# The last feed-forward product kept by tokens instead of by features, at the end of a two-block model

## The chip, the cores and the metric

The kernel runs on one core of a Trainium2 chip. Its metric is the device time of one execution in microseconds (us), the median of several runs. The core has five engines that run beside each other, each with its own queue in order: TensorE (PE in the profile, its weight loads PEld) multiplies matrices, VectorE (DVE) and ScalarE (ACT) work element by element, GpSimd (POOL) does a few small operations and issues some DMAs, SyncE (SP) issues most of the DMAs.

## The reference, cut to what matters

The model is two blocks on one sequence of 512 tokens with 1024 features, all in float32. Only the end of the second block is touched by the change:

```
h  = rms_norm(x, ffn_pre_g)
gt, up = split(h @ w_gate_up)            # 1024 -> 2 x 2816
f  = (silu(gt) * up) @ w_down            # 2816 -> 1024
x  = x + rms_norm(f, ffn_post_g)         # a norm per token over 1024 features
return x
```

## The kernel before, in words

**Layout.** Nearly everything is kept by features: a tile holds 128 features in its partitions and the 512 tokens in its columns, so 1024 features are eight tiles. The host hands in x transposed and transposes the output back (`outT`, 1024 x 512).

**Products.** A float32 product is done as three TensorE products of a rounded high part and a low part (`mm3`, lines 149 to 152). `gemm_tile` (line 154) makes one output tile of 128 features: for each 128 rows of the contraction it loads the weights as the stationary operand and passes the activations, 512 tokens wide, as the moving one. Weights come in blocks of up to 8 x 128 columns (`wblock`, line 143): SP loads the block to `wr`, ACT casts it to `wh` (line 138), DVE subtracts to get `wl` (line 139). There are three buffers each of `wr`, `wh` and `wl`. `gemm_tok` (line 180) is another form, used early in the kernel: there the activations are stationary, 128 tokens at a time, and the weights move, 512 columns wide.

**Order.** The program is written as one straight line and a planner (the tile framework) puts each engine's instructions in order by priority; weight blocks have a priority of 300 instructions ahead (`WPRI`). A buffer that is still in use makes the next writer wait in its engine's queue.

**The feed-forward part (lines 1089 to 1154).** The 44 tiles of gate and up take 24 matmuls each of 512 columns. Each pair gives one hidden tile (`hid`, high and low part `uh`, `ul`). The hidden tiles are made in two groups of eleven. After the first group eight output tiles get the first half of the contraction, 33 matmuls of 512 columns each, and are copied to `fo`. After the second group the token range is cut in two halves of 256: for each half the eight output tiles get the rest, 33 matmuls of 256 columns each, so each weight block of that group is loaded and split twice. Then comes the norm of the half: squares of the eight tiles are summed by ACT and DVE, `col_sum` (line 217) sums them over the partitions by small matmuls (line 223), `rsqrt_col` (line 227) gives one column per 128 tokens, the power on POOL (line 231), `row_bc` (line 234) spreads the columns to a row by four passes of TensorE (line 238), ACT copies it out (line 256), and two DVE operations per output tile (lines 1152 and 1153) scale it and add the residual `h`. The output leaves in 128 KB DMAs (line 1154). The norm of the first half is put off so that it lies beside the matmuls of the second.

Of the kernel before, what the change touches and what calls it, by code (L numbers as in the profile page):

```python
# [6 lines left out]
F32 = mybir.dt.float32  # L7
# [9 lines left out]
P = 128  # L17
S = 512
# [20 lines left out]
X1 = 0  # L39
X2 = 30  # L40
X3 = 40
TLATE = 30
APRI = 60
BPRI = 120

# [23 lines left out]
def _build(tc, nc, es, a, out):  # L69
# [58 lines left out]
    def vcol(name, i=0, n=1):  # L128
        c, k = VEC[name]
        assert i + n <= k  # L130
        return vec[:, c + i:c + i + n]
# [22 lines left out]
    def gemm_tile(src_blocks, xs, n=S):  # L154

        ps = acc.tile([P, S], F32, tag="acc", name="acc")
        k0, tot = 0, sum(nk for _, nk in src_blocks)
        for src, nk in src_blocks:
            wh, wl = wblock(src, nk)
            for k in range(nk):  # L160
                xh, xl = xs[k0]
                mm3(ps[:, :n], wh[:, k, :], wl[:, k, :], xh, xl, k0 == 0, k0 == tot - 1)
                k0 += 1
        return ps
# [43 lines left out]
    def sq_acc(accum, k, src, scale=1.0):  # L208
        if k == 0:
            A.activation(out=accum, in_=src, func=AF.Square, scale=scale)  # L210
        else:
            sq = nrm.tile([P, S], F32, tag="sq", name="sq")
            n = accum.shape[-1]
            A.activation(out=sq[:, :n], in_=src, func=AF.Square, scale=scale)
            V.tensor_tensor(out=accum, in0=accum, in1=sq[:, :n], op=ALU.add)
# [872 lines left out]

    with ExitStack() as ec:
        pc = ec.enter_context(pool("pf2", 2, reuse_waits="tile"))  # L1090
        ph2 = ec.enter_context(pool("phid2", 11, reuse_waits="tile"))
        fo = [None] * 8

        def gu_tiles(ns):

            pss, ws = [], []
            for n in ns:
                pss.append(acc.tile([P, S], F32, tag="acc", name="acc"))
                ws.append(wblock(a["w_gu"][n]))
            for cl in parts:  # L1100
                for ps, (wh, wl) in zip(pss, ws):
                    for k in range(8):
                        mm3(ps[:, cl], wh[:, k, :], wl[:, k, :], xs[k][0][:, cl], xs[k][1][:, cl], k == 0, k == 7)
            return pss

        order = [n for i in range(22) for n in (i, 22 + i)]

        early = {}
        for n, ps in zip(order, gu_tiles(order[:3]) + [gemm_tile([(a["w_gu"][n], 8)], xs) for n in order[3:NEARLY]]):
            early[n] = pc.tile([P, S], F32, tag=f"e{n}", name="early", bufs=1)  # L1110
            A.copy(out=early[n], in_=ps)
        for cl in parts:
            r3(cl, HF)

        def gu(n):
            return early[n] if n in early else gemm_tile([(a["w_gu"][n], 8)], xs)

        for grp in range(2):
            hid = []
            for n in range(11 * grp, 11 * grp + 11):  # L1120
                ps = gu(n)
                t = pc.tile([P, S], F32, tag="t", name="t")
                V.tensor_tensor(out=t, in0=ps, in1=R3, op=ALU.mult)
                A.activation(out=t, in_=t, func=AF.Silu)
                ps = gu(22 + n)
                t2 = pc.tile([P, S], F32, tag="t2", name="t2")
                V.tensor_tensor(out=t2, in0=ps, in1=R3, op=ALU.mult)
                V.tensor_tensor(out=t2, in0=t2, in1=t, op=ALU.mult)
                hid.append(split_act(t2, pl=ph2, tag="u"))
            o = grp * 11  # L1130
            if grp == 0:
                for n in range(8):
                    w = a["w_dn"][n]
                    ps = gemm_tile([(w[:, o:o + 8, :], 8), (w[:, o + 8:o + 11, :], 3)], hid)
                    fo[n] = pso.tile([P, S], F32, tag=f"so{n}", name=f"f{n}")
                    A.copy(out=fo[n], in_=ps)
                continue
            for hf in range(2):
                cl = slice(hf * HF, (hf + 1) * HF)
                hh = [(x[0][:, cl], x[1][:, cl]) for x in hid]  # L1140
                ac = nrm.tile([P, S], F32, tag="sqa", name="sqa")
                acs = [ac[:, :HF], ac[:, HF:]]
                for n in range(8):
                    w = a["w_dn"][n]
                    ps = gemm_tile([(w[:, o:o + 8, :], 8), (w[:, o + 8:o + 11, :], 3)], hh, HF)
                    V.tensor_tensor(out=fo[n][:, cl], in0=fo[n][:, cl], in1=ps[:, :HF], op=ALU.add)

                    sq_acc(acs[n // 7], n % 7, fo[n][:, cl])
                    A.activation(out=fo[n][:, cl], in_=fo[n][:, cl], func=AF.Copy, scale=vcol("ffn_post_g_2", n))
                Rf, _ = norm_fin(acs, D, 2, pl=pc, rtag="Rf", late=TLATE * (1 - hf))  # L1150
                for n in range(8):
                    V.tensor_tensor(out=fo[n][:, cl], in0=fo[n][:, cl], in1=Rf, op=ALU.mult)
                    V.tensor_tensor(out=fo[n][:, cl], in0=fo[n][:, cl], in1=h[n][:, cl], op=ALU.add)
                    nc.sync.dma_start(out=out[n * P:(n + 1) * P, cl], in_=fo[n][:, cl])


_OUT_SHAPE = (1, S, D)
# [2 lines left out]
def _pack(inp):  # L1160
    import numpy as np

    def fm(w):
        K, N = w.shape
        return np.ascontiguousarray(w.reshape(K // P, P, N // P, P).transpose(2, 1, 0, 3))

    def tm(w):
        K, N = w.shape
        return np.ascontiguousarray(w.reshape(K // 256, 2, P, N // S, S).transpose(3, 0, 2, 1, 4))

    g = {}
    i = {k: np.asarray(v) for k, v in inp.items()}
    g["xT"] = np.ascontiguousarray(i["x"][0].T)
    g["memT"] = np.ascontiguousarray(i["mem"][0].T)
    w = i["w_in"][0]
    o = [0, 512, 1024, 1536, 1544, 2056, 2568, 3080, 3592]
    p = [w[:, o[k]:o[k + 1]] for k in range(8)]
    g["w_fq"], g["w_fk"], g["w_fv"] = fm(p[0]), fm(p[1]), tm(p[2])[0]
    g["w_ff"] = np.pad(p[3].reshape(8, P, 8).transpose(1, 0, 2), ((0, 0), (0, 0), (0, 24)))
    g["w_gq"], g["w_gf"], g["w_gi"], g["w_gg"] = fm(p[4]), fm(p[5]), tm(p[6])[0], fm(p[7])  # L1180
    wo = i["w_out"][0]
    g["w_out"] = fm(np.concatenate([wo[512:], wo[:512]]))
    g["w_xq"], g["w_xo"], g["w1"], g["w2"] = fm(i["w_xq"][0]), fm(i["w_xo"][0]), fm(i["w1"][0]), fm(i["w2"][0])
    w = i["w_in_2"][0]
    g["w_glu"], g["w_z"], g["w_xs"] = fm(w[:, 0:2048]), fm(w[:, 2048:4096]), fm(w[:, 4096:6144])
    g["w_B"], g["w_C"], g["w_gate"] = fm(w[:, 6144:7168]), fm(w[:, 7168:8192]), fm(w[:, 8224:])
    g["w_dt"] = np.ascontiguousarray(w[:, 8192:8224].reshape(8, P, 32).transpose(1, 0, 2))
    g["w_pw"], g["w_so"], g["w_out2"] = fm(i["conv_pw_w_2"][0]), fm(i["ssm_out_w_2"][0]), fm(i["w_out_2"][0])
    g["w_gu"], g["w_dn"] = fm(i["w_gate_up_2"][0]), fm(i["w_down_2"][0])
    g["w_xk"], g["w_xv"] = fm(i["w_xkv"][0][:, :D]), tm(i["w_xkv"][0][:, D:])  # L1190

    vec = np.zeros((P, NVEC), np.float32)

    def put(name, arr):
        c, k = VEC[name]
        vec[:arr.shape[0], c:c + k] = arr

    for name, k in _VEC_SHAPES:
        v = i[name]
        if name == "conv_dw_w_2":  # L1200
            put(name, v[0].reshape(31, 8, P).transpose(2, 1, 0).reshape(P, 8 * 31))
        elif name == "ssm_conv_w_2":
            put(name, v[0].reshape(4, 32, P).transpose(2, 1, 0).reshape(P, 32 * 4))
        elif name == "d_skip_2":
            put(name, np.repeat(v[0], 64).reshape(16, P).T)
        elif name in ("fox_f_bias", "dt_bias_2", "a_log_2"):
            put(name, v[0].reshape(-1, 1))
        else:
            put(name, v.reshape(-1).reshape(k, P).T)
    g["vec"] = vec  # L1210

    r = np.arange(P)
    g["ident"] = np.eye(P, dtype=np.float32)
    g["tri"] = (r[:, None] <= r[None, :]).astype(np.float32)
    g["cmask"] = np.where(r[None, :] <= r[:, None], 0.0, NEG).astype(np.float32)
    lm = np.zeros((P, 7, 64), np.int32)
    for lv in range(7):
        n = 1 << lv
        t = r.reshape(-1, 2, n)[:, 1, :].reshape(-1)
        lm[:, lv, :] = (r[:, None] // (2 * n) == t[None, :] // (2 * n)) & (r[:, None] // n % 2 == 0)  # L1220
    g["lmask"] = lm
    return g
# [17 lines left out]
```

## Time and profile before

| | |
|---|---|
| runs | 1915.81, 1916.11, 1916.19 us; median 1916.11 |
| profiled execution | 1916.54 us |
| its span, first to last instruction | 1914.8 us |
| PE busy | 1892.4 us, 99% |
| DVE, ACT, POOL busy | 63%, 45%, 5% |
| granted TensorE clock | 0.997 of full |
| read from HBM | 198.71 MB |

The profile shows one execution. A matmul's shown length runs past the start of the next one, since they are pipelined; the distance between two starts is what a matmul takes. The other engines' lengths can be read as they stand.

### The profile page before, as it was taken

What the parts mean: (1) busy time and instruction counts of PE and PEld (TensorE: products, weight loads), DVE (VectorE), ACT (ScalarE), POOL (GpSimd) and SP (SyncE); (2) the same over time, 40 slices, a digit from 0 to 9 for tenths busy, and PEclk for the clock granted to TensorE, in tenths of its full rate; (3) what the DMA queues carried; (4) which work ended last, traced back from release to release, by engine and by line L of the source; (5) the groups of instructions that cost most, each with busy time, mean ns of one, the idle gap of its engine ahead of it and who ended that gap; (6) DMA issues with size and microseconds to landing.
All of it is one profiled execution on the core that took longest, in us unless ns stands there. A gap on an engine that the chain in (4) does not pass through costs nothing.

```text
span 1914.8 us, 25080 instructions
## 1 busy us (share of the span) xinstructions
PE 1892.4 (99%) x9680; PEld 1573.7 (82%) x9680; DVE 1207.1 (63%) x1886; ACT 861.7 (45%) x1393; POOL 101.8 (5%) x198
## 2 busy tenths in 40 slices
PE   9999999999999999999999999999999999999997
PEld 8887776877888888877888888888888988888897
DVE  6744756655443344467888989578997774324456
ACT  6524547444331233348545553545344653222344
POOL 1001110000000000011110110110000000000000
PEclk9999999999999999999999999999999999999999
DMA  7412212322323333344333333333345532233244
GB/s 259 132 57 86 67 54 80 100 66 78 94 95 98 99 99 104 110 95 142 119 122 108 108 119 105 107 115 103 102 141 186 165 91 98 83 116 98 90 130 145
DMA packets 67542, 208.84 MB, mean 109 GB/s; under 512 B 8536, under 2 KB 15448, under 8 KB 67424
## 3 DMA queue, kind: packets, MB, share of 16 engines
q1 hardware_dynamic: 57856, 184.09, 30.9%
q0 software_dynamic: 5968, 16.87, 3.0%
q10 hardware_dynamic: 3600, 6.30, 0.9%
q8 instruction: 76, 1.25, 0.3%
q14 instruction: 42, 0.34, 0.1%
HBM read 198.71 MB, written 8.54 MB: 108 GB/s over the span
## 4 chain that ended last, share of the span: by engine, by line
PE 51%; issue 2%; DVE 1%; DMA 1%; ACT 0%; POOL 0%; POOLq 0%; DVEq 0%; ACTq 0%
PE acc L150 16%; PE acc L151 16%; PE acc L152 16%; PE pb L916 1%; PE pa L886 1%; PE pc L238 0%; PE pa L878 0%; PE pa L868 0%; PE pc L223 0%; PE pa L238 0%; DMA ab<-acsd 0%; DMA wr<-w_dn 0%; PE pa L223 0%; POOL rc L231 0%; PE pa L861 0%
## 5 line engine op out<-in xcount | busy, mean ns | idle before, releaser
L138 ACT CAST wh<-wr 128x1024 fp32r<-128x1024 f32 (+1 forms) x343 | 347.1, 1013 | 714.7 <-PE acc L151 585.1
L139 DVE TENSOR_TENSOR wl<-wr,wh 128x1024 fp32r<-128x1024 f32 (+1 forms) x343 | 403.2, 1176 | 287.4 <-ACT wh L138 277.8
L150 PE MATMUL acc<-yh,wh 128*128 128x512 f32 (+1 forms) x1112 | 432.9, 390 | 0.1
L152 PE MATMUL acc<-yh,wl 128*128 128x512 f32 (+1 forms) x1112 | 431.2, 388 | 0.0
L151 PE MATMUL acc<-yl,wh 128*128 128x512 f32 (+1 forms) x1112 | 429.8, 387 | 0.0
L152 PE MATMUL acc<-xh,wl 128*128 128x512 f32 (+1 forms) x832 | 313.7, 377 | 0.3 <-DVE wl L139 0.3
L150 PE MATMUL acc<-xh,wh 128*128 128x512 f32 (+1 forms) x832 | 313.7, 378 | 0.3 <-DVE h L594 0.3
L151 PE MATMUL acc<-xl,wh 128*128 128x512 f32 (+1 forms) x832 | 313.1, 377 | 0.0
L150 PEld LDWEIGHTS acc<-yh,wh 128*128 128x128 f32 x1112 | 209.1, 188 | 42.0 <-issue 1.4
L152 PEld LDWEIGHTS acc<-yh,wl 128*128 128x128 f32 x1112 | 209.1, 188 | 40.9
L151 PEld LDWEIGHTS acc<-yl,wh 128*128 128x128 f32 x1112 | 209.1, 188 | 40.3 <-DVE yl L202 0.4
L150 PE MATMUL acc<-uh,wh 128*128 128x512 f32 (+1 forms) x520 | 183.9, 354 | 0.0
L151 PE MATMUL acc<-ul,wh 128*128 128x512 f32 (+1 forms) x520 | 183.7, 353 | 0.0
L152 PE MATMUL acc<-uh,wl 128*128 128x512 f32 (+1 forms) x520 | 183.6, 353 | 0.0
L807 DVE SCALAR_TENSOR_TENSOR cv<-gp,vec,cv 128x512 f32<-128x512 f32 x240 | 177.6, 748 | 6.0 <-ACT cv L805 3.0
L150 PEld LDWEIGHTS acc<-xh,wh 128*128 128x128 f32 x832 | 157.1, 189 | 29.3 <-issue 1.5
L152 PEld LDWEIGHTS acc<-xh,wl 128*128 128x128 f32 x832 | 157.2, 189 | 28.7 <-issue 1.8
L151 PEld LDWEIGHTS acc<-xl,wh 128*128 128x128 f32 x832 | 157.2, 189 | 27.0 <-issue 1.2
L152 PEld LDWEIGHTS acc<-uh,wl 128*128 128x128 f32 x520 | 98.3, 189 | 13.5
L150 PEld LDWEIGHTS acc<-uh,wh 128*128 128x128 f32 x520 | 98.3, 189 | 13.4
L151 PEld LDWEIGHTS acc<-ul,wh 128*128 128x128 f32 x520 | 98.4, 189 | 13.3
L231 POOL TENSOR_TENSOR rc<-rv,mhalf 128x4 f32<-128x4 f32 (+1 forms) x25 | 29.7, 1188 | 966.4 <-DVE rv L229 883.2
(364 smaller groups left out, 2111.8 us busy)
## 6 DMA issues: line engine op xcount, KB each, us to landing
wr<-w SPq DMA_DIRECT2D x64, 512.0 KB, 3.8
wr<-w_gu SPq DMA_DIRECT2D x44, 512.0 KB, 3.5
wr<-w_out SPq DMA_DIRECT2D x24, 512.0 KB, 3.5
wr<-w_dn SPq DMA_DIRECT2D x24, 512.0 KB, 3.6
wr<-w_xs SPq DMA_DIRECT2D x16, 512.0 KB, 3.5
wr<-w_glu SPq DMA_DIRECT2D x16, 512.0 KB, 3.5
ab<-acsd POOLq DMA_DIRECT2D x32, 256.0 KB, 3.6
wr<-w_z SPq DMA_DIRECT2D x16, 512.0 KB, 3.5
```

The lines of the kernel that those rows point to most:

```text
L138: A.copy(out=hi[:, :n], in_=raw[:, :n])
L139: V.tensor_tensor(out=lo[:, :n], in0=raw[:, :n], in1=hi[:, :n].bitcast(F32), op=ALU.subtract)
L150: T.matmul(out=ps, lhsT=lh, rhs=rh, start=start, stop=False)
L151: T.matmul(out=ps, lhsT=lh, rhs=rl, start=False, stop=False)
L152: T.matmul(out=ps, lhsT=ll, rhs=rh, start=False, stop=stop)
L231: G.tensor_tensor(out=r[:, :nt], in0=v[:, :nt], in1=mhalf[:, :nt], op=ALU.pow)
L807: yield V.scalar_tensor_tensor(out=o, in0=gp[:, t:t + S], scalar=cw(t), in1=o, op0=ALU.mult, op1=ALU.add)
L886: T.matmul(out=ps[:, 0:256], lhsT=Bt[:, c, :], rhs=xw[:, c].rearrange("p r d -> p (r d)"), start=True, stop=True)
L916: m = T.matmul(out=dst[r * 64:r * 64 + 64, c * P:(c + 1) * P], lhsT=lh, rhs=rh, start=True, stop=True)
```

## The change: what it does

- The hidden tiles are made in groups of twelve and ten.
- The last product is done by tokens (`down`): the hidden tiles are stationary, 128 tokens at a time, and the weights move, 512 features wide. Its result has 128 tokens in the partitions and 512 features in the columns, so a token's sum of squares is one column, which ACT's square gives as its accumulated output, and the norm needs no TensorE. The power stays on POOL, now on one column of 128.
- The output is laid out by tokens, and the host transposes nothing.
- The residual `h` has to be turned: DVE transposes each of its eight tiles in 32 x 32 blocks (`turn`), and four DMAs per tile write the blocks to a DRAM tensor `hTd`, 512 pieces of 128 bytes each; eight DMAs read it back by tokens (`turned`). The scratch tile of `turn` has two buffers. These DMAs are on POOL's queue.
- The gain `ffn_post_g` is spread over the partitions by two DMAs (`gB`).
- In the second group the first 512 features are finished first. The weights for the other 512 are then kept, all ten rows of 128, so that the four token tiles can be finished one after the other, each with its own norm and output.

```diff
-        for grp in range(2):
+        def turn(k):
+            t = nrm.tile([P, S], F32, tag="sq", name="ht")
+            V.transpose(out=t, in_=h[k])
+            for i in range(4):
+                c = k * P + i * 32
+                G.dma_start(out=hTd[:, c:c + 32].rearrange("(b i) j -> i b j", i=32),
+                            in_=t[i * 32:i * 32 + 32, :].rearrange("i (b j) -> i b j", j=32))
+        def turned():
+            for hf in range(2):
+                c = slice(hf * S, (hf + 1) * S)
+                G.dma_start(out=gB[hf], in_=a["post_g"][:, c].partition_broadcast(P))
+                for j in range(4):
+                    G.dma_start(out=hT[hf][j], in_=hTd[j * P:(j + 1) * P, c])
+        tk = lambda x, j: (x[0][:, j * P:(j + 1) * P], x[1][:, j * P:(j + 1) * P])
+        def down(hf, c0, hid):
+            pss = [acc.tile([P, S], F32, tag="acc", name="acc") for _ in range(3)] + [mC()] if hf == 0 else \
+                [mA(), mA(), mB(), mB()]
+            nk = len(hid)
+            for c in range(nk // 2):
+                wh, wl = wblock(a["w_dn"][hf][c0 + c], 2, S)
+                for j in range(4):
+                    for kk in range(2):
+                        k = 2 * c + kk
+                        mm3(pss[j], *tk(hid[k], j), wh[:, kk, :], wl[:, kk, :], k == 0, k == nk - 1)
+            return pss
...
                 hid.append(split_act(t2, pl=ph2, tag="u"))
+                if 2 <= n < 10:
+                    turn(n - 2)
+                elif n == 10:
+                    turned()
...
+        hid = hidden(range(12))
+        for hf in range(2):
+            for j, ps in enumerate(down(hf, 0, hid)):
+                fo[4 * hf + j] = pso.tile([P, S], F32, tag=f"so{4 * hf + j}", name=f"f{4 * hf + j}")
+                A.copy(out=fo[4 * hf + j], in_=ps)
+        hid = hidden(range(12, 22))
+        def squares(src, name):
+            t = pc.tile([P, S], F32, tag="t2", name="junk")
+            s = psm.tile([P, 1], F32, tag=name, name=name, bufs=4)
+            A.activation(out=t, in_=src, func=AF.Square, accum_out=s)
+            return s
+        for j, ps in enumerate(down(0, 6, hid)):
+            f = fo[j]
+            V.tensor_tensor(out=f, in0=f, in1=ps, op=ALU.add)
+            s = squares(f, "s0")
+            V.tensor_scalar(out=s, in0=s, scalar1=1.0 / D, scalar2=EPS, op0=ALU.mult, op1=ALU.add)
+            s0.append(s)
+            V.tensor_tensor(out=f, in0=f, in1=gB[0], op=ALU.mult)
+        ws = []
+        for c in range(5):
+            src = a["w_dn"][1][6 + c]
+            if c == 4:
+                wh, wl = wblock(src, 2, S)
+                ws += [(wh[:, kk, :], wl[:, kk, :]) for kk in range(2)]
                 continue
+            with tc.high_priority(WPRI):
+                raw = wraw.tile([P, 8 * P], F32, tag="wr", name="wr")
+                nc.sync.dma_start(out=raw, in_=src.rearrange("p k c -> p (k c)"))
+                for kk in range(2):
+                    ws.append(split_act(raw[:, kk * S:(kk + 1) * S], pl=pyn, tag="y"))
+        for j, ps in enumerate((mA(), mA(), mB(), mB())):
+            for k in range(10):
+                mm3(ps, *tk(hid[k], j), *ws[k], k == 0, k == 9)
+            f = fo[4 + j]
+            V.tensor_tensor(out=f, in0=f, in1=ps, op=ALU.add)
+            s = squares(f, "s1")
+            v = psm.tile([P, 1], F32, tag="v", name="v", bufs=2)
+            V.tensor_scalar(out=v, in0=s, scalar1=1.0 / D, scalar2=s0[j], op0=ALU.mult, op1=ALU.add)
+            r = psm.tile([P, 1], F32, tag="r", name="r", bufs=2)
+            G.tensor_tensor(out=r, in0=v, in1=mhalf[:, 0:1], op=ALU.pow)
+            t = pc.tile([P, S], F32, tag="t", name="fg")
+            V.tensor_tensor(out=t, in0=f, in1=gB[1], op=ALU.mult)
+            for hf, y in ((1, t), (0, fo[j])):
+                V.scalar_tensor_tensor(out=y, in0=y, scalar=r, in1=hT[hf][j], op0=ALU.mult, op1=ALU.add)
+                (nc.sync if hf else nc.scalar).dma_start(out=out[j * P:(j + 1) * P, hf * S:(hf + 1) * S], in_=y)
```

Beside these, the three `early` gate and up tiles move to buffers of the pool `act`, whose slots the residual by tokens and the gain use too, and `ph2` has twelve buffers for hidden tiles instead of eleven. The kept weights `ws` lie in the pool `pyn`, in the eight slots that the input of gate and up holds until their last tile is done.

## Rows read from the trace of the kernel before

**Rows 1.** The page's part 1: busy time, share of the span, instructions of each engine.
```profile
PE 1892.4 (99%) x9680; PEld 1573.7 (82%) x9680; DVE 1207.1 (63%) x1886; ACT 861.7 (45%) x1393; POOL 101.8 (5%) x198
```

**Rows 2.** Timeline of PE in the feed-forward part: start, length (us), instruction.
```profile
1657.32 0.39 PE L150 MATMUL acc<-uh,wh 128*128 128x512 f32 x1
...
1717.16 0.39 PE L150 MATMUL acc<-yh,wh 128*128 128x512 f32 x1
...
1836.84 0.28 PE L150 MATMUL acc<-uh,wh 128*128 128x256 f32 x1
...
1901.77 0.28 PE L152 MATMUL acc<-uh,wl 128*128 128x256 f32 x1
```

**Rows 3.** Timeline of PE in an early product by tokens.
```profile
53.23 0.39 PE L150 MATMUL acc<-wh,mh 128*128 128x512 f32 x1
...
57.77 0.39 PE L152 MATMUL acc<-wh,ml 128*128 128x512 f32 x1
```

**Rows 4.** Timeline of all engines behind the last product; brackets: idle before, releaser.
```profile
1902.09 0.42 DVE L1146 TENSOR_TENSOR f<-f,acc 128x256 f32<-128x256 f32 x1 [2.37 <-PE acc L152]
1902.54 0.42 ACT L210 ACTIVATE sqa<-f 128x256 f32<-128x256 f32 x1 [2.74 <-DVE f L1146]
...
1903.95 0.16 DVE L229 TENSOR_SCALAR rv<-pa 128x2 f32<-128x2 f32 x1 [1.44 <-PE pa L223]
1904.19 0.70 POOL L231 TENSOR_TENSOR rc<-rv,mhalf 128x2 f32<-128x2 f32 x1 [31.87 <-DVE rv L229]
...
1910.80 0.75 DVE L1153 TENSOR_TENSOR f<-f,x 128x256 f32<-128x256 f32 x2
```

**Rows 5.** Groups by line and shape: count | busy us, mean ns | idle before.
```profile
L960 DVE TENSOR_TENSOR so<-so,acc 128x512 f32<-128x512 f32 x8 | 5.4, 681 | 0.5 <-PE acc L152 0.5
L214 ACT ACTIVATE sq<-zs 128x512 f32<-128x512 f32 x8 | 5.1, 634 | 20.6 <-DVE zs L934 20.6
L517 ACT ACTIVATION_READ_ACCUMULATOR Sx<-Sx,nm 128x1 f32 x32 | 6.0, 187 | 0.0
L231 POOL TENSOR_TENSOR rc<-rv,mhalf 128x2 f32<-128x2 f32 x7 | 6.2, 887 | 483.4 <-DVE rv L229 483.4
L942 DVE SCALAR_TENSOR_TENSOR zs<-zs,vec,pc 128x512 f32<-128x512 f32 x16 | 11.7, 739 | 0.0
L901 POOL DMA_DIRECT2D ab<-acsd x32 | 18.0, 563 | 59.7 <-ACT mt L906 56.8 <-ACT ab L905 2.8 <-DVE xt L784 0.2
L114 POOL DMA_DIRECT2D mt<-memT x2 | 1.6, 823 | 0.8 <-POOLq L1230 0.8
L139 DVE TENSOR_TENSOR wl<-wr,wh 128x1024 fp32r<-128x1024 f32 x77 | 94.1, 1223 | 49.4 <-ACT wh L138 48.7 <-PE acc L151 0.7
L138 ACT CAST wh<-wr 128x1024 fp32r<-128x1024 f32 x76 | 79.9, 1052 | 169.2 <-PE acc L151 100.4 <-issue 59.1 <-DMA wr<-w_dn 7.7
```

**Rows 6.** DMA issues of the whole span: count, KB each, median us to landing.
```profile
wr<-w_dn SPq DMA_DIRECT2D x24, 512.0 KB, 3.6
...
gated<-gt ACTq DMA_DIRECT2D x16, 256.0 KB, 2.0
...
outT<-f SPq DMA_DIRECT2D x16, 128.0 KB, 1.8
```

**Rows 7.** Stage of the first gate and up tiles: length, busy us of each engine, clock, DMA share, GB/s.
```profile
1570.00:1657.00 87.00, 87.00 (x385) 72.03 (x385) 41.59 (x52) 26.78 (x34) 0.00 (x0) 1.00 0.29 90
```

**Rows 8.** DMA issues between 850 and 861 us.
```profile
wr<-w_glu SPq DMA_DIRECT2D x2, 512.0 KB, 8.4
eacd<-s__6619 POOLq DMA_DIRECT2D x1, 64.0 KB, 9.0
cdd<-s__6619 POOLq DMA_DIRECT2D x1, 0.5 KB, 10.5
```

**Rows 9.** Waits of ACT between 1480 and 1916: us in total, times, longest.
```profile
ACT wh L138 <- PE acc L151: 148.2, 72, 3.9
...
ACT wh L138 <- DMA wr<-w_dn: 7.7, 7, 1.9
```

More of the change, by code (lines that the diff above doesn't have):

```diff
@@ L41 @@
 X3 = 40
-TLATE = 30
 APRI = 60
@@ L1090, in _build @@
         pc = ec.enter_context(pool("pf2", 2, reuse_waits="tile"))
-        ph2 = ec.enter_context(pool("phid2", 11, reuse_waits="tile"))
+        ph2 = ec.enter_context(pool("phid2", 12, reuse_waits="tile"))
+        psm = ec.enter_context(pool("psm", 1, reuse_waits="tile"))
         fo = [None] * 8
@@ L1109, in _build @@
         for n, ps in zip(order, gu_tiles(order[:3]) + [gemm_tile([(a["w_gu"][n], 8)], xs) for n in order[3:NEARLY]]):
-            early[n] = pc.tile([P, S], F32, tag=f"e{n}", name="early", bufs=1)
+            early[n] = act.tile([P, S], F32, tag="xl", name="early")
             A.copy(out=early[n], in_=ps)
@@ L1116, in gu, with hidden @@
             return early[n] if n in early else gemm_tile([(a["w_gu"][n], 8)], xs)
-        for grp in range(2):
+        hTd = dram.tile([S, D], F32, tag="hTd", name="hTd")
+        hT = [[act.tile([P, S], F32, tag="xh", name="hT") for _ in range(4)] for _ in range(2)]
+        gB = [act.tile([P, S], F32, tag="xl", name="gB") for _ in range(2)]
+        def turn(k):
[23 more added lines that the diff above has]
+            return pss
+        def hidden(ns):
             hid = []
-            for n in range(11 * grp, 11 * grp + 11):
+            for n in ns:
                 ps = gu(n)
@@ L1129, in _build @@
                 hid.append(split_act(t2, pl=ph2, tag="u"))
[L1130 to L1136, printed above, removed]
-                continue
[L1138 to L1154, printed above, removed]
@@ new lines, in hidden @@
+                if 2 <= n < 10:
+                    turn(n - 2)
+                elif n == 10:
+                    turned()
+            return hid
+        hid = hidden(range(12))
[4 more added lines that the diff above has]
+        hid = hidden(range(12, 22))
+        s0, s1, junk = [], [], []
+        def squares(src, name):
[3 more added lines that the diff above has]
+            return s
@@ L1188, in _pack @@
     g["w_pw"], g["w_so"], g["w_out2"] = fm(i["conv_pw_w_2"][0]), fm(i["ssm_out_w_2"][0]), fm(i["w_out_2"][0])
-    g["w_gu"], g["w_dn"] = fm(i["w_gate_up_2"][0]), fm(i["w_down_2"][0])
+    g["w_gu"], g["w_dn"] = fm(i["w_gate_up_2"][0]), tm(i["w_down_2"][0])
+    g["post_g"] = i["ffn_post_g_2"].reshape(1, D)
     g["w_xk"], g["w_xv"] = fm(i["w_xkv"][0][:, :D]), tm(i["w_xkv"][0][:, D:])
@@ L1233 @@
         args[name] = nc.dram_tensor(name, arr.shape, mybir.dt.from_np(arr.dtype), kind="ExternalInput").ap()
-    out = nc.dram_tensor("outT", (D, S), F32, kind="ExternalOutput").ap()
+    out = nc.dram_tensor("out", (S, D), F32, kind="ExternalOutput").ap()
     with tile.TileContext(nc) as tc:
@@ L1238 @@
     import numpy as _np
-    return _np.ascontiguousarray(r.results[0]["outT"].T).reshape(_OUT_SHAPE)
+    return r.results[0]["out"].reshape(_OUT_SHAPE)
```

## The prediction

> **What bounds the kernel now.** I read the page's busy shares first, then the timeline of PE around the last product, then the timeline of all engines behind it, then the groups and DMA issues that give prices for the new work. PE is busy for 99% of the span [rows 1], and its matmuls follow each other without a gap, so time is gained only where PE needs fewer microseconds, or behind its last matmul, where everything stands in line.
>
> The reader is to see the stages in [rows 2] as starts of PE. From 1657.32 to 1717.16 lie the 264 matmuls of 512 columns of the first half: 59.84 us, 0.2267 each. To 1836.84 lie the 528 matmuls of the second eleven gate and up pairs: 119.68 us, again 0.2267. There is no stall in either. From 1836.84 to the end of the last slot (1901.77 and one slot of 0.12, 1901.89) lie 528 matmuls of 256 columns and the norm of the first token half: 65.05 us. The starts there are 0.12 apart where nothing is between them: 528 x 0.12 is 63.36, and the other 1.69 us are the small matmuls of that norm and the gaps round them. The last product has thus cost 59.84 + 65.05 = 124.89 us of PE.
>
> **The change on PE.** By tokens it is 12 + 10 rows of the contraction, two halves of the features, four token tiles, three products: 528 matmuls, all of 512 columns. That the form by tokens has the same rate is to be seen early in the kernel: from 53.23 to 57.77 are 20 matmuls with activations stationary and weights moving, 0.227 each [rows 3]. So 528 x 0.2267 = 119.68 us, 5.21 less: 3.52 from the width (two of 256 take 0.24, one of 512 takes 0.2267, 264 times) and 1.69 from the norm, which needs no TensorE any more. The end of PE's last slot moves from 1901.89 to 1896.68. The gate and up tiles are the same 44, only cut 12 and 10.
>
> The Trainium skill (TensorE: Matmul & The Clock Gate, Back-to-back issue gap) gives 262 cycles for 256 columns and 518 for 512, so by it the width is worth only 6 cycles at 2.4 GHz, 264 times, 0.7 us as an estimate, and the time would be 2.8 us more than my sum. The starts in the timeline (0.12 and 0.2267 us) show wider gaps than it gives, at the full granted clock, and they decide.
>
> **The change behind the last matmul.** Before, the last DVE operation ends at 1910.80 + 0.75 = 1911.55, 9.66 us after PE's last slot [rows 4]: an addition, a square, sums and spreading by PE, the power, a copy, and sixteen DVE operations. After, for the last token tile: the addition starts 0.20 behind the slot, as before (1902.09 against 1901.89); it takes 0.68 for 512 columns [rows 5]; 0.03 to ACT (1902.09 + 0.42 to 1902.54); the square 0.63, and its accumulated output is a second instruction of 0.19; about 0.05 to DVE (my guess, between the 0.03 and 0.08 of the other hops); 0.16 for the small operation [rows 4]; 0.08 to POOL; the power; 0.05; then two DVE operations of 0.74, the second starting some 0.07 before the first has ended, so 1.41. The power on one column is not in the trace. Two columns took 0.70 in the tail [rows 4] and 0.89 in the mean [rows 5]; one costs no more than two and at least nothing; I take 0.60, near the tail's own row. The multiplication by the gain lies beside the square. Sum: 0.20 + 0.68 + 0.03 + 0.82 + 0.05 + 0.16 + 0.08 + 0.60 + 0.05 + 1.41 = 4.08. The last DVE operation ends at 1896.68 + 4.08 = 1900.76, 10.79 us earlier than before.
>
> Behind that, before, came an output DMA, its landing and the closing semaphores: 1911.55 to the span's end 1914.8, 3.25 us. The last two DMAs now carry 256 KB each instead of 128. Landing is 2.0 us for 256 KB written from ACT's queue and 1.8 for 128 KB [rows 6], so at least 0.2 more; two at once could add as much as a whole landing, 2.0. I take 0.3, near the row, since the first leaves 0.7 us ahead. The span becomes 1914.8 - 10.79 + 0.3 = 1904.3. The profiled execution took 1916.54, 1.74 over its span, and lies 0.43 over the median of the runs: 1904.3 + 1.74 - 0.43 = **1905.6 us**.
>
> **What I cost at nothing, and its cover.** *The eight DVE transposes.* No such operation is in the trace; they cost at least nothing, and at most a few times the 1.22 of the largest subtraction [rows 5]; I take the 0.68 of an ordinary pass. In the stage where they go, DVE is busy for 41.6 of 87 us [rows 7], so either way it has room: one goes with each pair of gate and up tiles, 48 x 0.2267 = 10.88 us of PE. *The 42 DMAs on POOL.* POOL has nothing else in that stage (0.00 busy [rows 7]), and the powers at the end come far later. An issue is 0.56 us for 128 pieces and 0.82 for 256 [rows 5], so 2 ns per further piece; 512 pieces make about 1.35, four of them 5.4 per transposed tile, half of the 10.88 at hand. The read-back waits on POOL's queue for the last writes; nothing stands behind it there until the powers some 100 us later. *The smaller weight traffic.* The second group's weights come once instead of twice. It only frees engines that were not the bound. *The kept weights.* They may be split once the last gate and up tile has freed the slots in `pyn`, and the first features of the second group cover this with 120 matmuls, 120 x 0.2267 = 27.2 us. In it four kept blocks and one ordinary one must land and be split behind the last two ordinary ones. ACT mostly waits for PE, to give buffers back (148.2 us in 72 waits), and for the weights' DMA only 7.7 us in 7 [rows 9]; at 3.6 us from issue to landing [rows 6] and three loads at a time that leaves room. *PSUM.* The third accumulator of a new product is needed 12 matmuls (2.72 us) after the last gate and up matmul, and DVE frees it with one pass of 0.68, at worst behind a subtraction of 1.22.
>
> **Rival 1, slower: the writes of the turned residual hold DVE.** The scratch tile has two buffers, so transpose k stands in DVE's queue until the four writes of k - 2 have landed, and behind it stand the subtractions of the weights and the passes that empty PSUM. Let the writes of one tile take D, one tile after another. Transpose 7 is due 7 x 10.88 = 76.2 us after transpose 0 and can't start before 6 x D. PE is covered for two blocks of weights less a cast and a subtraction (1.05 and 1.22 [rows 5]): 10.88 - 2.27 = 8.6 us. PE is late by 6 x D - 84.8, and the kernel gets slower than before from D = 15.9 us, 4 us per DMA. For it: the only DMA of the trace that writes small pieces to DRAM, `cdd` with 128 pieces of 4 bytes, took 10.5 us to land, with two weight loads beside it at 8.4 [rows 8] instead of 3.6. At 10.5 a DMA, D is 42 us, PE is late by 167, and the time is 2073, the upper bound. Against it: `eacd`, 64 KB in whole rows of 2 KB issued just before, took 9.0 in the same place, so at most 1.5 of the 10.5 need be the small pieces; and the writes of a tile overlap each other. With the issue as the limit D is 5.4 and a landing, some 8 us, and the lower bound is no delay. A moderate D of 20 us gives 35 us late, 1941. Chance 0.14.
>
> The Trainium skill (DMA: Bandwidth & Descriptors, Measured) states about 10.5 ns per packet where packets are small, and calls for 512 bytes a piece at least. By that, as an estimate, 512 pieces take 5.4 us, D is 21.5, and the time would be 1950. It is a case of rival 1. None of the trace's DMAs is made of 128-byte pieces, so no run here shows it yet.
>
> **Rival 2, the kept weights come late.** Two ordinary blocks are used up 10.9 us into the cover, and the last ordinary one is split 2.3 us later. If each of the four blocks left then is loaded only behind the split before it (3.6 to land, 2.3 to split) instead of three at a time, the last is ready at 13.2 + 4 x 5.9 = 36.8. It is due at 27.2 + 5.4 = 32.6: a stall of 4.2 us, and 1910. For it: this stretch asks for ten blocks in 27 us, and they share three `wr` buffers. Against it: the waits for DMA in [rows 9] were short when more was loaded per microsecond. Chance 0.08.
>
> **Rival 3, the gains are eaten.** A DVE or weight delay of about 10 us, rival 1 with D near 15.8, gives 1916 and no difference. It needs D in a narrow place. Chance 0.05.
>
> **How the numbers follow.** My forecast has 0.73: 1905.6, by itself from 1904 (the power and the landing at their low ends) to 1908 (a mean power, two landings in line). The range of all reaches up past rival 2, to 1913, and leaves out rivals 1 and 3. A difference of 0.2%, 3.8 us, is about what can be told from no change: faster (below 1912.3) is my forecast and rival 2, 0.81; the same is rival 3, 0.05; slower is rival 1, 0.14.
>
> **What would show it.** PE: 528 matmuls of 512 columns on `uh` and `ul`, 0.2267 apart, no 256 wide ones, and no rows of lines 223 and 238 in the last product. The tail from PE's last slot to the last DVE operation near 4.1 us instead of 9.7, with POOL near 0.6 in it. The writes to `hTd` landing in some 2 to 4 us; if they land in over 4, DVE should show waits at the transposes, and PE waits at `wl` of line 139 in the gate and up stage, and rival 1 holds. PE waiting at the first kept weights would be rival 2. The forecast is wrong if PE's starts by tokens lie more than 0.23 apart, or if any gap of PE stands between 1570 and the end.

## The result and the profile after

The changed kernel takes 1905.65 us (median of 4 runs, 1904.66 to 1906.01); the kernel before took 1916.15 beside it (4 runs, 1915.81 to 1917.48). The ratio is 0.9943, 95% interval 0.9926 to 0.9960. The profiled execution took 1906.01 with a span of 1904.2. Line numbers behind the removed constant `TLATE`, which put off the first norm, are one lower than before.

The page's part 1 of the changed kernel, against [rows 1]:

```profile
span 1904.2 us, 24376 instructions
...
PE 1885.8 (99%) x9392; PEld 1556.8 (82%) x9392; DVE 1193.3 (63%) x1842; ACT 840.1 (44%) x1353; POOL 128.6 (7%) x242
```

PE is still busy for 99%. Its stages, from the timeline of PE, against [rows 2]; the columns are start, length in us, instruction, and the first row is the start of the 256-wide stage ahead of the feed-forward part:

```profile
1484.38 0.28 PE L149 MATMUL acc<-xh,wh 128*128 128x256 f32 x1
...
1668.61 0.39 PE L149 MATMUL acc<-wh,uh 128*128 128x512 f32 x1
...
1733.89 0.39 PE L149 MATMUL acc<-yh,wh 128*128 128x512 f32 x1
...
1842.69 0.39 PE L149 MATMUL acc<-wh,uh 128*128 128x512 f32 x1
...
1869.89 0.39 PE L149 MATMUL pa<-yh,uh 128*128 128x512 f32 x1
...
1896.86 0.39 PE L151 MATMUL pb<-wh,ul 128*128 128x512 f32 x1
```

The reader is to see 288 matmuls in the first group (65.28 us, 0.2267 each), 480 for the ten later pairs (108.80), and 120 each for the two halves of the second group (27.20 and 27.20). Nothing is lost between them, and the last stretch with the kept weights begins on time. Of PE's waits from 1480 us to the end one row is left, and it belongs to a norm, not to the feed-forward products:

```profile
PE pa L237 <- POOL rc L230: 1.1, 2, 0.6
```

The 256-wide stage begins at 1484.38, and at 1483.98 in the kernel before:

```profile
1483.98 0.28 PE L150 MATMUL acc<-xh,wh 128*128 128x256 f32 x1
```

Up to there every engine does the same operations in the same order in both, so the 0.40 us by which the changed kernel is behind are scatter as far as can be told: in a second execution of it this start is 1487.10, and over all profiled executions it lies between 1481.87 and that. From there to the end of PE's last slot it is 1896.86 + 0.23 - 1484.38 = 412.71 us, against 417.91 before. What lies behind the last slot, from the timeline of all engines, against [rows 4]; brackets give the idle time before and what ended it:

```profile
1897.29 0.69 DVE L1211 TENSOR_TENSOR f<-f,pb 128x512 f32<-128x512 f32 x1 [2.91 <-PE pb L151]
...
1898.07 0.63 ACT L1183 ACTIVATE junk<-f 128x512 f32<-128x512 f32 x1 [6.08 <-DVE f L1211]
1898.61 0.19 ACT L1183 ACTIVATION_READ_ACCUMULATOR junk<-f 128x1 f32 x1
1898.83 0.21 DVE L1214 TENSOR_SCALAR v<-s,s 128x1 f32<-128x1 f32 x1
1899.18 0.54 POOL L1216 TENSOR_TENSOR r<-v,mhalf 128x1 f32<-128x1 f32 x1 [6.25 <-DVE v L1214]
1899.76 0.75 DVE L1220 SCALAR_TENSOR_TENSOR fg<-fg,r,hT 128x512 f32<-128x512 f32 x1 [0.72 <-POOL r L1216]
1900.43 0.75 DVE L1220 SCALAR_TENSOR_TENSOR f<-f,r,hT 128x512 f32<-128x512 f32 x1
```

From the slot's end, 1897.09, to the last DVE operation's end, 1901.18, are 4.09 us, against 9.66; this is the tail from here on. From there to the end of the span are 3.0, against 3.2. So the span's 10.6 us are +0.40 ahead of the change, -5.20 on PE, -5.57 in the tail and -0.2 behind it.

The turn, as groups by line (count | busy us, mean ns | idle before) and as DMA issues (count, KB each, median us to landing), against [rows 5, 6]:

```profile
L1126 DVE STREAM_TRANSPOSE ht<-x 128x512 f32<-128x512 f32 x8 | 5.5, 699 | 0.0
L1129 POOL DMA_DIRECT2D hTd<-ht x32 | 20.7, 653 | 24.1 <-DVE ht L1126 22.0 <-issue 2.1
```

```profile
hTd<-ht POOLq DMA_DIRECT2D x32, 64.0 KB, 2.7
hT<-hTd POOLq DMA_DIRECT2D x8, 256.0 KB, 6.0
...
out<-f ACTq DMA_DIRECT2D x4, 256.0 KB, 2.1
```

And the same window as [rows 7], with the same columns:

```profile
1570.00:1657.00 87.00, 87.00 (x385) 72.06 (x384) 46.18 (x59) 27.38 (x35) 19.69 (x32) 1.00 0.45 138
```

DVE has 46.2 us to do instead of 41.6, POOL 19.7 instead of nothing, the transfers' share rises from 0.29 to 0.45, and PE does not notice.

### The profile page after: what moved, and what is told of

Its sections match the earlier page's. It is cut to its first block, busy times and chain, and to the rows that moved or that the text cites. A ratio compares the mean times of both kernels' runs of the same rounds, so it can differ in the third digit from the quotient of the medians.

```text
span 1904.2 us, 24376 instructions
## 1 busy us (share of the span) xinstructions
PE 1885.8 (99%) x9392; PEld 1556.8 (82%) x9392; DVE 1193.3 (63%) x1842; ACT 840.1 (44%) x1353; POOL 128.6 (7%) x242
## 3 DMA queue, kind: packets, MB, share of 16 engines
q0 software_dynamic: 7792, 21.59, 3.9%
## 4 chain that ended last, share of the span: by engine, by line
PE 53%; issue 1%; DVE 0%; ACT 0%; DMA 0%; POOL 0%; DVEq 0%; POOLq 0%; ACTq 0%
PE acc L149 15%; PE acc L151 15%; PE acc L150 15%; PE pb L915 1%; PE pa L885 1%; PE pb L151 1%; PE pa L151 1%; PE pb L149 1%; PE pa L149 1%; PE pb L150 1%; PE pa L150 1%; PE pc L237 0%; PE pa L877 0%; PE pa L867 0%; DMA ab<-acsd 0%
## 5 line engine op out<-in xcount | busy, mean ns | idle before, releaser
L137 ACT CAST wh<-wr 128x1024 fp32r<-128x1024 f32 x313 | 328.6, 1051 | 694.9 <-PE acc L150 514.2
L138 DVE TENSOR_TENSOR wl<-wr,wh 128x1024 fp32r<-128x1024 f32 x313 | 382.6, 1223 | 280.4 <-ACT wh L137 270.7
L149 PE MATMUL acc<-uh,wh 128*128 128x512 f32 x256 | 99.6, 389 | 0.0
L150 PE MATMUL acc<-ul,wh 128*128 128x512 f32 x256 | 99.6, 389 | 0.0
L151 PE MATMUL acc<-uh,wl 128*128 128x512 f32 x256 | 99.6, 389 | 0.0
L680 DVE SCALAR_TENSOR_TENSOR t<-acc,R 128x512 f32<-128x512 f32 x32 | 22.0, 691 | 79.5 <-PE acc L151 78.5
L149 PEld LDWEIGHTS acc<-uh,wh 128*128 128x128 f32 x256 | 48.0, 188 | 10.1
L150 PEld LDWEIGHTS acc<-ul,wh 128*128 128x128 f32 x256 | 48.0, 188 | 9.9
```

Of the source, the lines that this page charges most:

```text
L137: A.copy(out=hi[:, :n], in_=raw[:, :n])
L138: V.tensor_tensor(out=lo[:, :n], in0=raw[:, :n], in1=hi[:, :n].bitcast(F32), op=ALU.subtract)
L149: T.matmul(out=ps, lhsT=lh, rhs=rh, start=start, stop=False)
L150: T.matmul(out=ps, lhsT=lh, rhs=rl, start=False, stop=False)
L151: T.matmul(out=ps, lhsT=ll, rhs=rh, start=False, stop=stop)
L680: V.scalar_tensor_tensor(out=t, in0=ps, scalar=0.0, in1=R, op0=ALU.max, op1=ALU.mult)
```

## The experiments

Each was timed beside the kernel before, in three groups; before was 1916.01, 1915.90 and 1916.58 us in them.

**The width alone, by features.** The kernel before with the second group's last product 512 tokens wide and one norm at the end (the `early` tiles move to pool `act`, as in the change, to make room):

```
-            for hf in range(2):
-                cl = slice(hf * HF, (hf + 1) * HF)
...
+            for n in range(8):
+                w = a["w_dn"][n]
+                ps = gemm_tile([(w[:, o:o + 8, :], 8), (w[:, o + 8:o + 11, :], 3)], hid)
...
+            Rf, _ = norm_fin(ac, D, 4, pl=pc, rtag="Rf")
```

> The kernel before, with one thing done alone: the second half of the last product is not cut in token halves, so it is 264 matmuls of 512 columns instead of 528 of 256; results stay by features and the norm comes once, for all 512 tokens, at the end. Theory (the gain is 3.5 us of width and 1.7 of a norm taken off PE, and the rest, some 5.4, is the short tail that only tokens in the partitions allow): PE's last slot ends 5.2 us earlier, but the tail from it to the last DVE operation grows from 9.7 to about 17 (addition, square and sum 2.0, sums and power 2.1, spreading and copy 1.6, hops 0.4, sixteen DVE operations of 0.69 make 11.0), so 1918 us (1915 to 1920), no gain. Rival (the width of the matmuls is the gain): 1911.

Measured: 1918.61 us (11 runs), ratio 1.0013, 1.0005 to 1.0022. PE's stretch is 412.71 us, as in the changed kernel, so its 5.2 us come from the width and the norm's place, by features as by tokens. But the tail is long. The timeline behind the last slot (1897.32):

```profile
1899.74 1.02 PE L223 MATMUL pa<-ones,sqa 128*128 128x1 f32 x8 [2.26 <-DVE sqa L215]
...
1902.17 2.07 PE L238 MATMUL pa<-ident,rc 128*128 128x128 f32 x8 [1.41 <-POOL rc L231]
...
1913.34 1.29 DVE L1148 TENSOR_TENSOR f<-f,x 128x512 f32<-128x512 f32 x2
```

It ends at 1914.63, 17.31 us behind the slot against 4.09. What PE gave was handed back at the end; by tokens it is kept.

**No turn.** The changed kernel without transposes and writes; the residual's read-back takes a weight instead:

```
-                    G.dma_start(out=hT[hf][j], in_=hTd[j * P:(j + 1) * P, c])
+                    G.dma_start(out=hT[hf][j], in_=a["w_gu"][4 * hf + j].rearrange("p k c -> p (k c)")[:, 0:S])
...
-                if 2 <= n < 10:
-                    turn(n - 2)
-                elif n == 10:
+                if n == 10:
```

> The changed kernel without the turned residual: the eight DVE transposes and the 32 writes to DRAM are left out, and the read-back takes the same number of bytes from a weight tensor, so what is added at the end is not the residual. Theory (the turn costs nothing, DVE and the DMA engines have room): 1905.6, within 0.7 us; PE without gaps as before. Rival (the turn takes DVE time and DMA share that PE feels): 1 to 5 us faster, 1901 to 1904.5.

Measured: 1909.68 us (6 runs, 1908.25 to 1910.80). Both theories missed: with work taken out it is 4 us slower. PE's stretch is 412.73 us, as in the changed kernel, and the tail 4.37, 0.28 longer since POOL's power started later in this execution; most of the loss lies behind the last DVE operation, 7.7 us against 3.0. The waits of SP at the end (total, times, longest us):

```profile
SPq L1300 <- PEq L1300: 5.3, 2, 4.8
SPq L1300 <- DMA out<-fg: 1.3, 1, 1.3
SPq L1300 <- DMA out<-f: 0.6, 1, 0.6
```

In the changed kernel the first of these rows has 0.7 in all. The view names PE's queue, but PE had long been done; the instructions of the kernel's closing line tell who was late. The row to look at is DRAIN, an instruction with which each engine's queue closes. A view by line (duration ns min/median/max, first and last start); first this kernel, then the changed one, then the kernel before:

```profile
L1300 POOLq DRAIN  x3: 51/102/8911, 1898.9 to 1908.3; - x3
...
L1300 PEldq DRAIN  x2: 13/2139/4265, 1892.5 to 1908.1; - x2
```

```profile
L1303 POOLq DRAIN  x3: 46/93/1643, 1899.2 to 1903.9; - x3
```

```profile
L1235 POOLq DRAIN  x3: 46/93/8260, 1904.2 to 1914.5; - x3
```

POOL's longest drain starts with its last power, which lies inside it, and takes 8.91 us without the turn and 1.64 with it. In the kernel before it took 8.26 too, from 1904.15 to 1912.41, but there DVE worked until 1911.55 and the outputs landed later still, so nobody saw it. Without the turn it ends at 1907.8, when the last output has been there since 1902.96 and SP has waited since 1903.2; the span ends 0.8 later.

**POOL's own instructions in place of the writes.** To the kernel without the turn, 40 memsets of one column are added:

```
+        pad = psm.tile([P, 1], F32, tag="pad", name="pad", bufs=1)
...
+                if 2 <= n < 10:
+                    for _ in range(5):
+                        G.memset(pad, 0.0)
```

> The kernel without the turn (no transposes, no writes, the residual read back from a weight instead, so the output isn't the reference's), with 40 one-column memsets put on POOL where the 32 writes stood. Without the turn POOL's closing drain took 8.91 us (1898.88 to 1907.79) against 1.64 us in the changed kernel, and the whole of the 4 us loss lies there. Theory A (POOL's place in its own instruction stream decides, so any 40 instructions of it do what the writes did): drain 1.6 us, 1905.6 us as the changed kernel. Theory B (the transfers that POOL's queue has issued decide): memsets change nothing, drain 8.9 us, 1909.7 us.

Measured: 1909.46 us (6 runs), the drain 8.91 us: theory B. How many instructions POOL has had is not the reason.

**The writes without the transposes.**

```
-            t = nrm.tile([P, S], F32, tag="sq", name="ht")
-            V.transpose(out=t, in_=h[k])
+            t = h[k]
```

> The changed kernel with the eight transposes left out and the 32 writes kept (they write the residual as it lies, so the output isn't the reference's). Theories A and B alike: POOL's queue is as in the changed kernel, its closing drain 1.6 us, 1905.6 us; the transposes' 8 x 0.70 us on DVE hide beside PE, so the time differs by less than 0.7 us. If the transposes are what shortened the ending, the drain is 8.9 us and the time 1909.7 us; if they cost their own length, 1900 us.

Measured: 1905.28 us (5 runs), PE's stretch 412.71, and the drain 1.48 us:

```profile
L1302 POOLq DRAIN  x3: 46/93/1480, 1899.4 to 1904.2; - x3
```

The transposes neither cost anything nor shorten the ending; the 32 writes do that.

**The writes on SP's queue.**

```
-                G.dma_start(out=hTd[:, c:c + 32].rearrange("(b i) j -> i b j", i=32),
+                nc.sync.dma_start(out=hTd[:, c:c + 32].rearrange("(b i) j -> i b j", i=32),
```

> The changed kernel with the turn's 32 writes issued on SP's queue instead of POOL's; everything else as it is. Theory (POOL's closing drain goes by the transfers that POOL's own queue has issued, and without the 32 it is long): POOL has issued 101 transfers as in the two kernels without writes, drain 8.9 us from about 1899, so 1909.7 us although PE's last slot ends where it did. Rival (the writes' traffic shortens it, from whatever queue): drain 1.6 us, 1905.6 us. If SP's queue, which holds the weights, is held up by writes that wait for their transpose, PE shows waits on weights and the time is above both.

Measured: 1910.46 us (5 runs, 1908.48 to 1911.06). The same line of the closing view:

```profile
L1303 POOLq DRAIN  x3: 51/93/8912, 1899.6 to 1909.0; - x3
```

The same bytes moved from another queue, and the drain is long. PE's stretch (412.69) is untouched, so whatever the writes held up in SP's queue did not reach PE. It is what POOL's queue has issued that counts.

**As many writes, in whole rows.** No transposes, and 32 pieces of 2 KB per write instead of 512 of 128 bytes:

```
+        hTr = hTd.rearrange("s (e d) -> (s e) d", d=S)
...
-            V.transpose(out=t, in_=h[k])
+            t = h[k]
...
-                G.dma_start(out=hTd[:, c:c + 32].rearrange("(b i) j -> i b j", i=32),
-                            in_=t[i * 32:i * 32 + 32, :].rearrange("i (b j) -> i b j", j=32))
+                G.dma_start(out=hTr[c:c + 32, :], in_=t[i * 32:i * 32 + 32, :])
```

> The changed kernel without the transposes, with the 32 writes on POOL's queue as whole rows of 2 KB (32 pieces each) instead of 512 pieces of 128 bytes; the output isn't the reference's. Theory (the number of transfers that POOL's queue issued decides): drain 1.6 us, 1905.3 us as with the small pieces. Rival (the small pieces, 16384 of them, decide): drain 8.9 us, 1909.5 us.

Measured: 1905.60 us (5 runs), drain 1.64 us. The size of the pieces is not the reason either. The number of writes, their bytes and the profile's count of packets on POOL's queue (7792) are the same in both kernels, so this run does not tell those apart.

**Every write six times.**

```
-        hTd = dram.tile([S, D], F32, tag="hTd", name="hTd")
+        hTds = [dram.tile([S, D], F32, tag=f"hTd{e}", name=f"hTd{e}") for e in range(6)]
+        hTd = hTds[0]
...
+                for d in hTds:
+                    G.dma_start(out=d[:, c:c + 32].rearrange("(b i) j -> i b j", i=32),
...
```

> The changed kernel with every write of the turn done six times, to six DRAM tensors: 24 issues x 0.65 = 15.6 us of POOL's queue per tile and 3 us to the landing, D = 18.6 us. The first rival's sum in the prediction (DVE held by the tile that is still being written; slower from D = 15.9 us, 1941 at 20) gives 1932 us. My theory: the order of DVE's work is set with the writes' length in it, and the transposes come later and further apart, so nothing waits: PE's last slot ends where it did (1896.9), 1905.6 us, +-0.7 if POOL's closing drain stays at 1.6 us, 1910 if the 160 more transfers make it long.

Measured: 1905.31 us (5 runs); PE's stretch 412.69, drain 3.11 us, ended before the last output had landed. The first rival's 1932 did not come. The transposes and the drain in the view by line:

```profile
L1305 POOLq DRAIN  x3: 46/93/3113, 1899.7 to 1904.4; - x3
...
L1127 DVE STREAM_TRANSPOSE ht<-x x8: 669/704/706, 1557.7 to 1790.4; 128x512 f32<-128x512 f32 x8
```

In the changed kernel they lie from 1557.2 to 1600.1. Here they are spread over 233 us instead of 43, and DVE's order itself is another: between the second and the third transpose stand 29 other operations of DVE, against 14 in the changed kernel. So the planner, which sets that order, moved them apart; whether by the length of the writes or by their number is not shown. POOL waits for the transposes (122.9 us), and DVE has no wait for POOL's writes.

**The last stretch in narrow matmuls.** Its 120 matmuls of 512 columns as 240 of 256:

```
-            for k in range(10):
-                mm3(ps, *tk(hid[k], j), *ws[k], k == 0, k == 9)
+            for e in range(2):
+                q = slice(e * HF, (e + 1) * HF)
+                for k in range(10):
+                    wh, wl = ws[k]
+                    mm3(ps[:, q], *tk(hid[k], j), wh[:, q], wl[:, q], k == 0, k == 9)
```

> The changed kernel with the last product's 480 matmuls of 512 columns for the second half done as 960 of 256, same weights and same data, so that each 512 of the before's rate (0.2267 us) becomes two of 0.120 us as in its two last feature tiles: PE's stretch gets 480 x 0.0133 = 6.4 us longer if all of the second half's last product were so, and the part changed here is the 120 accumulated triples of four tiles (4 x 10 x 3 = 120 matmuls of 512), so 120 x 0.0133 = 1.6 us: 1907.2 us by the rows of before (theory: width alone costs this). By the issue gap that the Trainium skill gives (TensorE: Matmul & The Clock Gate, Back-to-back issue gap), 6 cycles a pair, 0.3 us: 1905.9 us (rival).

Measured: 1907.37 us (5 runs, 1906.20 to 1908.27). The last matmuls of its timeline lie 0.12 apart:

```profile
1897.49 0.28 PE L150 MATMUL pb<-wl,uh 128*128 128x256 f32 x1
1897.61 0.28 PE L151 MATMUL pb<-wh,ul 128*128 128x256 f32 x1
```

The stage ahead began at 1483.43, so the stretch is 414.30 us, 1.59 longer: 0.0133 a pair, by the rows of before. (The 480 and 6.4 us in the expectation are a slip: the second group has 240 such matmuls. The 120 that were changed are counted rightly.)

**The last weights not kept.** The last half block by block, as the others:

```
-        for j, ps in enumerate((mA(), mA(), mB(), mB())):
-            for k in range(10):
-                mm3(ps, *tk(hid[k], j), *ws[k], k == 0, k == 9)
+        for j, ps in enumerate(down(1, 6, hid)):
```

> The changed kernel without the kept weights: the last 512 features of the second group go like the other three products, weight block by weight block over all four token tiles, so the four tiles end within 4 us of each other instead of 6.8 us apart. Theory (keeping the weights spreads the norms, additions and outputs over PE's last 27 us): PE's last slot unchanged at about 1897, the four tiles' DVE work of 3.0 us each (two passes of 0.69, one of 0.21, two of 0.71) stands in line from 3.9 us before the last slot, so the last DVE operation is about 8.1 us behind it instead of 4.1, and 1909.6 us (1908 to 1911). Rival (the tail is set by one tile's chain, whatever is in front): 1905.6.

Measured: 1910.13 us (6 runs). PE's stretch is the same; the four token tiles end within some 4 us of each other, and their ends stand in line on DVE:

```profile
1901.58 0.68 DVE L1197 TENSOR_TENSOR f<-f,pb 128x512 f32<-128x512 f32 x1
...
1904.72 0.75 DVE L1206 SCALAR_TENSOR_TENSOR f<-f,r,hT 128x512 f32<-128x512 f32 x1
```

The last tile's addition starts 5.5 us behind the slot's end (1896.11) instead of 0.2, and the tail is 9.36 us. Keeping the weights is worth 5.3 us of tail and costs PE nothing. Against the 9.66 us of the kernel before, the result by tokens without it would have shortened the tail by 0.3 us only: by tokens the end can be short, and the order makes it so.

**The last half's first sums held in PSUM.** Four accumulators stay open over the second group, with no copy and no addition:

```
-        for hf in range(2):
-            for j, ps in enumerate(down(hf, 0, hid)):
...
+        held = down(1, 0, hid, False)
...
-            f = fo[4 + j]
-            V.tensor_tensor(out=f, in0=f, in1=ps, op=ALU.add)
+            f = ps
```

> The changed kernel, with one step of its tail taken out: the four token tiles of the last 512 features stay in their PSUM banks after the first group, and the second group goes on adding to them, so they are neither copied out nor added up, and ACT squares and DVE scales straight from PSUM. Theory (the tail is one chain, every operation of it counts in full): the addition of 0.69 and a hop go, the tail is 3.4 us instead of 4.1, and 1904.9 us. Rival (the end is set by something beside this chain, such as the output DMAs or ACT's queue): 1905.6.

Measured: 1904.93 us (5 runs). It was run again beside the changed kernel on one chip:

> The kernel with the last half's sums held in PSUM once more, beside the changed kernel on one chip: its tail from PE's last slot to the last op of DVE was 3.32 us against 4.09 in the changed kernel, the rest alike, so 0.8 us below the changed kernel: 1904.9 us if that is 1905.6. Rival: no difference.

> The changed kernel itself once more, on the same chip as the kernel with the held sums: 1905.6 us, POOL's closing drain 1.6 us. Rival (the short drain is an accident of one execution): 8.9 us and 1909.7 us.

Measured: 1902.86 us (5 runs, 1902.45 to 1905.37) against 1905.41 (5 runs, 1905.11 to 1908.75), ratios to before 0.9933 (0.9921 to 0.9946) and 0.9944 (0.9931 to 0.9958). The intervals overlap. What the traces show is the shorter tail, 3.32 and 3.33 us against 4.09 in both executions of the changed kernel; in it ACT squares straight from PSUM (the first of the two executions):

```profile
1897.23 0.39 PE L151 MATMUL pb<-wh,ul 128*128 128x512 f32 x1
...
1897.72 0.60 ACT L1183 ACTIVATE junk<-pb 128x512 f32<-128x512 f32 x1 [6.11 <-PE pb L151]
...
1900.04 0.74 DVE L1219 SCALAR_TENSOR_TENSOR fg<-fg,r,hT 128x512 f32<-128x512 f32 x1
```

Of the 0.77 us 0.1 is lost again behind it: from the slot's end to the end of the span are 6.5 us against 7.1, so 0.65 us are shown. Most of what the second pair of executions differs by is not from the edit: the 256-wide stage, ahead of all that differs, began at 1481.87 and 1487.10 in them. With 0.65 us shown by traces, though not by times alone, this is the best version run. The short drain of the changed kernel is there again (1.65 us).

## Why the prediction was right, and where only its number was

**PE.** Predicted -5.21 us, measured -5.20. That the width counts, and by how much, is shown by undoing it for one stretch (1.59 us for 120 pairs, 1.60 expected); 264 pairs make 3.5 at that rate, and the 1.7 left are the norm of the first token half, which the kernel by features, with the same stretch, has moved out of it too. The 6 cycles a pair that the Trainium skill's issue gap gives (TensorE: Matmul & The Clock Gate, Back-to-back issue gap) would be 0.3 there; the traces do not agree with it.

**The tail.** Predicted 4.08 us, measured 4.09. The chain of operations is the one forecast, but that the sum is right to 0.01 is luck, since five of its terms were off by 0.05 to 0.09 and cancelled: the hop to ACT 0.09 instead of 0.03, the hop to POOL 0.14 instead of 0.08, the small DVE operation 0.21 instead of 0.16; against these the square with its accumulated output 0.73 instead of 0.82 (the second instruction starts before the first has ended) and the power 0.54 instead of 0.60. The kernel in which the weights are not kept shows that this tail hangs on the order of the last product: one token tile after another.

**Behind the tail.** Predicted 3.55, measured 3.0. The two 256 KB outputs landed in 2.0 to 2.1 us each, without a price for being two; the last was there 2.1 us behind the last DVE operation, 1.9 before, so the 0.2 of the row was right. What follows the last landing took 1.0 us instead of 1.3, which I did not forecast and whose cause is open. And here the number came out without its whole reason. The 3.25 of before was an output's landing and semaphores, as I took it, but I did not see POOL's closing drain beside it: 8.26 us, hidden under a tail that ended at 1911.55. The change starts that drain at 1899.16 and takes its cover away. At 8.3 to 8.9 us it would have ended at 1907.4 to 1908.1, and as without the turn the span would have ended some 0.8 later: about 1910 us, not 1905.6 and outside the 1904 to 1908 of the forecast. It did not, because the turn's 32 writes, which I had costed at nothing, left the drain at 1.64 us. That was luck. Three kernels without these writes on POOL's queue show the other case (1909.68, 1909.46, 1910.46). And the 0.5 us too much behind the tail and the 0.40 by which this execution was late ahead of the change nearly cancel in the span, 1904.3 forecast and 1904.2 measured.

**What I costed at nothing** cost nothing. The transposes took 0.70 us each (0.68 taken). A write's issue took 0.65, not the 1.35 that I stretched from two rows; it landed in 2.7. Third accumulator and kept weights: no wait of PE.

**Rival 1** had no ground. Four issues and a landing make D 4 x 0.65 + 2.7 = 5.3 us; from the end of a transpose to the last landing of its tile the trace has 4.5 to 9.3, where the kernel would have become slower from 15.9. Single writes took up to 5.3 us, over the 4 that I had named as a sign, and still no transpose waited (0.0 idle). The rival's mechanism was wrong too. I let the transposes be due one per pair; in fact the planner put all eight within 43 us, and with six times the writes it put them further apart, so that a D of 17.3 to 20.7 us (36.6 for the second tile, whose writes stand behind the first's) cost nothing.

My estimate of a D of 21.5 took the 10.5 ns per packet of the Trainium skill (DMA: Bandwidth & Descriptors, Measured), which are given for reads from HBM, once for each of 512 pieces. That does not hold here: these writes were landed 2.7 us after the issue (median) and not 5.4, and in whole rows 2.2. On POOL's queue a piece is not a packet. The profile counts as many packets there with 512 pieces a write as with 32 (the changed kernel, then the one with whole rows):

```profile
q0 software_dynamic: 7792, 21.59, 3.9%
...
q0 software_dynamic: 7792, 21.59, 3.9%
```

The same writes on SP's queue are 16896 packets more there, 528 a write (the changed kernel, then the one with the writes on SP's queue), and landed in 3.7 us:

```profile
q1 hardware_dynamic: 52384, 177.27, 27.5%
...
q1 hardware_dynamic: 69280, 179.37, 29.7%
```

**Rival 2** did not come: the last stretch began without a gap. **Rival 3** neither.

## What to carry to other kernels

A layout that keeps a norm's sum within the engine's own rows pays above all at the end of a kernel: here the width and the norm's place won 5.2 us of PE either way, but by features 7.7 were given back in the tail and by tokens 5.6 more were won there. The layout alone hardly shortens the end: the last product has to finish one tile after another, too (5.3 us of tail). Before a tail is cut, look at the closing line of the profile for what the long tail hides; a drain on another engine can become the end. And if a kernel from which work was removed gets slower, compare the closing drains of all queues before the compute.

## What the runs showed of the hardware

- POOL's closing drain goes by what POOL's own queue has issued, and not in one direction: 8.26 to 8.91 us after 91 or 101 transfers (the kernel before and four others), 1.48 to 1.65 after 133 (six kernels), 3.11 after 293. Piece size, the same traffic from another queue, the transposes and the number of POOL's instructions are excluded. The number of transfers was never changed without their bytes and packets, and the 32 that shorten the drain are all writes to DRAM, so which of these matters, and why, stays open.
- 32 writes of 64 KB in 128-byte pieces took 0.65 us of POOL's queue each and landed in 2.2 to 5.3 us (median 2.7); in 2 KB pieces 0.50, and 1.9 to 3.8 (median 2.2). By the profile's count such a write is 32 packets on POOL's queue whatever its pieces (7792 in all, against 6768 without the 32 writes), and 528 on SP's with the 128-byte pieces.
- PE's stretch from the 256-wide stage to its end was the same within 0.04 us in twelve executions of ten kernels whose last product is 512 wide; the scatter of several us between executions lies ahead of that stage.
